# A two-layer hybrid encoder on one core: two gate/up tiles moved into the output projection, a norm weight moved to ScalarE, and the column halves of a product put in sequence

## The chip, the cores and the metric

The kernel runs on one core of a Trainium2 chip, in one launch, in float32. The metric is the device time of that core in microseconds, as the median of the runs. Matrix products run on TensorE (PE) with their weights loaded ahead of each matmul (PEld), results land in PSUM banks and are taken out by VectorE (DVE) or ScalarE (ACT). GpSimd (POOL) works on SBUF only, and SyncE (SP) issues most DMAs.

## The reference, cut to what matters

```python
for l in range(DEPTH):                                   # DEPTH = 2
    h = h + hybrid_mixer(rmsnorm(h, norm1_w[l]), ...)    # ends in: mix @ w_out
    h = h + swiglu(rmsnorm(h, norm2_w[l]), w_gate_up[l], w_down[l])
h = rmsnorm(h, final_norm_w)

def swiglu(h, w_gate_up, w_down):
    gate, up = jnp.split(h @ w_gate_up, 2, axis=-1)
    return (jax.nn.silu(gate) * up) @ w_down
```

The model width is 1024, the sequence 1024 plus 16 meta tokens, and gate and up are 2816 wide each. The change lies between the output projection of a layer (`mix @ w_out`) and the end of its gate/up products.

## The kernel before, in words

Activations are kept transposed: 128 channels on the partitions, tokens (1040 of them, 1024 in the last layer) along the free dimension. Every float32 operand is split in two float32r parts, hi and lo, and a product is three matmuls (hi by hi, hi by lo, lo by hi; lines 156 to 158 in `dense`, 1064 to 1066 in `prod`). For weights, ScalarE copies the raw tile to hi and GpSimd subtracts to get lo (lines 129, 130 in `wsplit`; 1046, 1047 in `w_op`).

**Output projection, second part.** `out_part(z, m)` adds one 128-channel block m of 8 for one half z of the token columns: 24 matmuls, two evacuations by VectorE (line 909, in `add_h`), a square on ScalarE and an add to the sums of the norm (line 954), and a store of the residual `hd`. `out_part(0, m)` runs for all m, then `out_part(1, m)`. Beside the latter, two blocks behind, VectorE forms the operands of the gate/up products.

**Gate and up as a Strassen-like product.** The operand (1024 channels by the tokens) is cut into four blocks B11, B21 (ready after z = 0) and B12, B22, and the weights of a tile f of 22 into A11, A12, A21, A22. Seven products follow: P1 (A11 B11), P2 (A12 B21), P3 (S4 B22), P4 (A22 T4), P5 (S1 T1), P6 (S2 T2), P7 (S3 T3). T1 to T4 are sums of the blocks, made by `t_sum` (line 981) and split into hi and lo by `t_split` (line 969) and `t_split_w` (line 177). S1 to S4 are sums of the weight blocks, made on VectorE for each tile (lines 1277, 1278, 1281, 1282). The norm weight of channels 0 to 511 in half z = 1 is multiplied in by a VectorE instruction of its own (line 1005).

**Early tiles.** P1 and P2 need only B11 and B21. For tiles 0 to 3 (`NE = 4`) they are done ahead, after all of the output projection, while VectorE finishes T1 to T4.

**The order within a tile.** In layer 0 the 520 columns of a half do not fit one bank, so each product runs twice (j = 0, 1) with 260 columns, 12 matmuls a time. The code runs all seven products for j = 0 and then all for j = 1. In the last layer one group of 12 matmuls of 512 columns is a product (`NJ = 1`). Bank c takes P5, is read by VectorE (line 1300), and then accumulates P3 on top. Bank b takes P6 (line 1314), P7 (line 1318) and P4 (line 1327) in this way, bank a P1 and P2. A product that accumulates therefore waits until VectorE has read the bank. After P4, gate and up are scaled and multiplied (line 1341 on GpSimd, 1342 and 1344 on VectorE).

**What sets the order.** A scheduler at build time places the instructions of each engine in one fixed order by the program's priorities and its own estimates; on the chip each engine then works through its list and waits by semaphores. So TensorE's list already interleaves products of neighbouring tiles. VectorE's list mixes evacuations with the sums of weights for the next tile.

Of the kernel before, what the change touches and what calls it, by code (L numbers as in the profile page):

```python
# [15 lines left out]
KT = 8  # L16
# [26 lines left out]
def trunk(ctx: ExitStack, tc: tile.TileContext, xT, w_in, w_ba, w_out, w_gu, w_dn,  # L43
# [235 lines left out]
    for l in range(DEPTH):  # L279
# [705 lines left out]
        X0, X1 = hb  # L985
        T = {}

        for m in range(KT):
            out_part(0, m)
            if m > 0:  # L990
                if m in (1, 5):
                    T[("B11", "B21")[m // 4]] = t_tile((Y[0][0], X[0][2])[m // 4])
                t_split_w(T[("B11", "B21")[(m - 1) // 4]], m - 1, 0)
        for m in range(KT + 2):
            if m < KT:
                out_part(1, m)
            if m == 0:
                t_split_w(T["B21"], 7, 0)
            k = m - 2
            if k < 0:  # L1000
                continue
            if k < 4:
                if k == 0:
                    T["T1"] = t_tile(Y[0][2])
                ts(out=hx(k, 1), in0=hx(k, 1), scalar1=pcol(P_N2 + k), scalar2=None, op0=ALU.mult)
                t_sum(k, 0, hx(k, 0), npar[:, k:k + 1], hx(k, 1), ALU.add)
                if k % 2:
                    t_split(T["T1"], X0, 0, k - 1)
            else:
                c = pcol(P_N2 + k)  # L1010
                if k == 4:
                    T["B22"] = t_tile(Y[0][1])
                t_split_w(T["B22"], k, 1)
                t_sum(k - 4, 1, hx(k, 1), c, hx(k - 4, 1))
                t_sum(k, 1, hx(k, 1), c, hx(k - 4, 0))
                t_sum(k, 0, hx(k, 0), c, hx(k, 1))
        T["T2"] = t_tile("P0")
        T["T3"] = t_tile("P1")
        for k in (0, 2):
            t_split(T["T2"], X1, 1, k)  # L1020
        for k in (0, 2):
            t_split(T["T3"], X0, 1, k)
        T["T4"] = t_tile(X[0][0])
        for k in (0, 2):
            t_split(T["T4"], X1, 0, k)

# [60 lines left out]
        NE = 4  # L1087
        early = {}
        for f in range(NE):
# [10 lines left out]
            for j in range(NJ):  # L1100
                prod(ab[j], w2, T["B21"], j, False)
                act(out=part(g, 0, j), in_=pin(ab[j]), func=AF.Copy)

# [163 lines left out]
        for f in range(FT):  # L1267
# [68 lines left out]
            else:  # L1336
                for j in range(NJ):
                    for p in (p1, p5, p3, p6, p7, p2, p4):
                        p(j)
# [214 lines left out]
```

## Time and profile before

| | us |
|---|---|
| median of 3 runs (2590.4 to 2598.9) | 2592.36 |
| profiled execution, its own time | 2589.49 |
| its span, first to last instruction | 2587.7 |
| TensorE busy | 2504.7 |
| VectorE busy | 1640.2 |
| GpSimd busy | 1134.3 |
| ScalarE busy | 1047.0 |

TensorE is busy for 97% of the span, so the time is that of its work plus its waits. The output projection's second half (z = 1) starts at 585.6 us in layer 0, the gate/up tiles run from there to about 1050 us; in the last layer the same stages lie from 1871.9 us to about 2360 us. In a row of a group, the numbers behind the bar are busy time and mean duration in ns, then the idle time just ahead and what ended it. In a row of waits they are the sum, the number of times and the longest.

### The profile page before, as it was taken

Reading aid. Unit: us, or ns where it says so; the run is one execution under the profiler, and the core shown is the slowest. Engines: PE = TensorE matmul, PEld = TensorE weight load, DVE = VectorE, ACT = ScalarE, POOL = GpSimd, SP = SyncE. Lnnn points to the kernel's source line nnn. Section 1 sums busy time; section 2 is a strip of 40 time slices with the busy share of each in tenths; the row PEclk is TensorE's granted clock in tenths of the full one; section 3 lists DMA queues with packets and bytes.
Section 4 is the critical chain, followed back from the end, with each engine's and each line's share of the span. In section 5 each row is a group of like instructions: output and inputs, shape, how many; then the busy total and the mean of one; then the engine's idle time right before and its main releaser. Section 6 shows DMA issues by size and latency. Waiting matters only on the chain. (4 is left out here: it accounts for less than half of the span.)

```text
span 2587.7 us, 45312 instructions
## 1 busy us (share of the span) xinstructions
PE 2504.7 (97%) x17508; PEld 2289.3 (88%) x17508; DVE 1640.2 (63%) x2461; ACT 1047.0 (40%) x1945; POOL 1134.3 (44%) x869
## 2 busy tenths in 40 slices
PE   8999999999899999999999989999989999999998
PEld 6989999998899999999998978999977778887787
DVE  4588433648766665778455874235587776668754
ACT  5563332435233333444445633324442333333444
POOL 2041212335666666665320302212456776774662
PEclk9999999999999999999999999999999999999999
DMA  3457265524422222674224582556343322228631
GB/s 127 128 184 266 92 206 167 186 78 124 131 98 87 96 83 81 212 221 144 78 92 134 189 269 77 181 159 204 106 133 115 111 88 92 89 82 276 202 109 66
DMA packets 213765, 360.04 MB, mean 139 GB/s; under 512 B 25461, under 2 KB 87869, under 8 KB 213549
## 3 DMA queue, kind: packets, MB, share of 16 engines
q1 hardware_dynamic: 180300, 310.17, 36.8%
q10 hardware_dynamic: 31072, 42.61, 5.4%
q0 software_dynamic: 2176, 4.36, 0.5%
q8 instruction: 137, 2.24, 0.4%
q14 instruction: 80, 0.65, 0.1%
HBM read 266.60 MB, written 90.46 MB: 138 GB/s over the span
## 5 line engine op out<-in xcount | busy, mean ns | idle before, releaser
L130 POOL TENSOR_TENSOR wlo<-raw,whi 128x512 fp32r<-128x512 f32 x132 | 177.5, 1346 | 770.2 <-ACT whi L129 698.4
L156 PE MATMUL pacc<-a,whi 128*128 128x346 f32 (+1 forms) x808 | 264.8, 331 | 9.9 <-ACT whi L129 8.3
L158 PE MATMUL pacc<-a,wlo 128*128 128x346 f32 (+1 forms) x808 | 264.5, 329 | 0.8 <-DVE wlo L130 0.8
L156 PE MATMUL pacc<-b,whi 128*128 128x346 f32 (+2 forms) x672 | 234.8, 350 | 0.0
L158 PE MATMUL pacc<-b,wlo 128*128 128x346 f32 (+2 forms) x672 | 232.5, 348 | 0.0
L157 PE MATMUL pacc<-a,whi 128*128 128x346 f32 (+1 forms) x688 | 227.0, 330 | 0.6 <-DVE a L177 0.3
L129 ACT ACTIVATE whi<-raw 128x512 fp32r<-128x512 f32 x168 | 105.2, 629 | 246.9 <-PE pacc L157 157.1
L157 PE MATMUL pacc<-b,whi 128*128 128x346 f32 (+2 forms) x580 | 200.5, 347 | 0.2 <-DVE b L905 0.2
L1047 POOL TENSOR_TENSOR wlo<-rw,whi 128x512 fp32r<-128x512 f32 x92 | 134.8, 1467 | 72.1 <-ACT whi L1046 66.8
L156 PEld LDWEIGHTS pacc<-a,whi 128*128 128x128 f32 x808 | 154.0, 191 | 13.9 <-ACT whi L129 10.2
L158 PEld LDWEIGHTS pacc<-a,wlo 128*128 128x128 f32 x808 | 154.1, 191 | 2.8 <-DVE wlo L130 1.4
L156 PEld LDWEIGHTS pacc<-b,whi 128*128 128x128 f32 x672 | 127.0, 189 | 11.4 <-issue 3.1
L157 PEld LDWEIGHTS pacc<-a,whi 128*128 128x128 f32 x688 | 131.8, 192 | 5.1 <-issue 2.9
L1047 POOL TENSOR_TENSOR a<-rw,a 128x512 fp32r<-128x512 f32 x64 | 105.6, 1651 | 69.7 <-ACT a L1046 69.0
L158 PEld LDWEIGHTS pacc<-b,wlo 128*128 128x128 f32 x672 | 126.9, 189 | 8.8 <-issue 0.8
L1047 POOL TENSOR_TENSOR b<-rw,b 128x512 fp32r<-128x512 f32 x64 | 92.6, 1449 | 84.2 <-ACT b L1046 50.2
L1046 ACT ACTIVATE whi<-rw 128x512 fp32r<-128x512 f32 x92 | 57.8, 630 | 144.5 <-DVE rw L1281 84.9
L157 PEld LDWEIGHTS pacc<-b,whi 128*128 128x128 f32 x580 | 109.6, 189 | 7.4 <-DVE b L905 0.5
L1282 DVE TENSOR_TENSOR rw<-raw,rw 128x512 f32<-128x512 f32 x44 | 97.2, 2209 | 1.2
L1277 DVE TENSOR_TENSOR rw<-rw,rw 128x512 f32<-128x512 f32 x44 | 67.5, 1533 | 47.3 <-POOL wlo L1047 30.9
L1047 POOL TENSOR_TENSOR wlo<-raw,whi 128x512 fp32r<-128x512 f32 x50 | 79.9, 1600 | 32.0 <-ACT whi L1046 21.3
L1046 ACT ACTIVATE b<-rw 128x512 fp32r<-128x512 f32 x64 | 40.2, 630 | 121.7 <-PE pacc L1065 35.2
(973 smaller groups left out, 8425.1 us busy)
## 6 DMA issues: line engine op xcount, KB each, us to landing
raw<-in_w_in SPq DMA_DIRECT2D x112, 256.0 KB
raw<-in_w_gu SPq DMA_DIRECT2D x104, 256.0 KB
rw<-in_w_gu SPq DMA_DIRECT2D x88, 256.0 KB
rw<-in_w_dn SPq DMA_DIRECT2D x86, 192.0 KB
rec<-aqd SPq DMA_DIRECT2D x62, 256.0 KB
rec<-vkd SPq DMA_DIRECT2D x61, 256.0 KB
raw<-in_w_out SPq DMA_DIRECT2D x48, 256.0 KB
b<-ad SPq DMA_DIRECT2D x45, 260.0 KB
```

The lines of the kernel that those rows point to most:

```text
L129: act(out=hi, in_=raw[:, 0:kk, :], func=AF.Copy)
L130: (tt if lov[0] else ptt)(out=lo, in0=raw[:, 0:kk, :], in1=hi.bitcast(F32), op=ALU.subtract)
L156: mm(ps[:, :n], wh, xh[:, n0:n1], start=(k == 0), stop=False)
L157: mm(ps[:, :n], wh, xl[:, n0:n1], start=False, stop=False)
L158: mm(ps[:, :n], wl, xh[:, n0:n1], start=False, stop=(k == K - 1))
L1046: act(out=hi, in_=src, func=AF.Copy)
L1047: ptt(out=lo, in0=src, in1=hi.bitcast(F32), op=ALU.subtract)
L1277: tt(out=s1t, in0=A21, in1=A22, op=ALU.add)
L1282: tt(out=A21, in0=A11, in1=A21, op=ALU.subtract)
```

## The change

Four edits, all between the output projection and the end of gate/up:

- The helper functions from `ad` to `pin` (unchanged) stand further up, and the body of the loop over early tiles becomes `early_tile(f)`. Tiles 0 and 1 are called in the loop over `out_part(1, m)`, right after m = 3 and m = 5. Tiles 2 and 3 stay where all four were.
- The norm weight (line 1005 before, 1087 after) is an activation with a scale on ScalarE.
- In a tile that is not the last, the loop over products is the outer one and the loop over column halves the inner one, and P2 stands ahead of P7.
- The split of A12 stands ahead of that of S3.

```diff
+        EARLY_AT = (3, 5)
+        def early_tile(f):
+            A11, A12 = raw4("raw"), raw4("raw")
+            dma(A11, w_gu[l, f, 0, :, 0:4, :])
+            dma(A12, w_gu[l, f, 0, :, 4:8, :])
+            w1, w2 = w_op(A11, True), w_op(A12, True)
...
         for m in range(KT + 2):
             if m < KT:
                 out_part(1, m)
+            if m in EARLY_AT:
+                early_tile(EARLY_AT.index(m))
...
-                ts(out=hx(k, 1), in0=hx(k, 1), scalar1=pcol(P_N2 + k), scalar2=None, op0=ALU.mult)
+                act(out=hx(k, 1), in_=hx(k, 1), func=AF.Copy, scale=pcol(P_N2 + k))
                 t_sum(k, 0, hx(k, 0), npar[:, k:k + 1], hx(k, 1), ALU.add)
...
-        for f in range(NE):
-            A11, A12 = raw4("raw"), raw4("raw")
...
+        for f in range(len(EARLY_AT), NE):
+            early_tile(f)
...
-                         [("S4", s2t), ("S3", A21), ("A12", A12), ("A22", A22)]):
+                         [("S4", s2t), ("A12", A12), ("S3", A21), ("A22", A22)]):
...
-                for j in range(NJ):
-                    for p in (p1, p5, p3, p6, p7, p2, p4):
+                for p in (p1, p5, p3, p6, p2, p7, p4):
+                    for j in range(NJ):
                         p(j)
```

Lines behind the moved block stand 7 further down in the changed kernel: 1277, 1278, 1281, 1282, 1300, 1311, 1314 become 1284, 1285, 1288, 1289, 1307, 1318, 1321, and 1318, 1327, 1342, 1344, 1347 become 1325, 1334, 1349, 1351, 1354.

What the scheduler makes of it is shown at three places on VectorE. The first is layer 0, where the last operands are done and tile 0 begins. The first piece is of the kernel before. P_ and a_671 are the splits of T2 to T4, rw tiles are sums of weights (6565 and 6558 of tile 0, 6736, 6737 and 6730 of tile 1), and a_680 is the up row of tile 0.

```order
L969 TENSOR_TENSOR a_671_6267<-a_511_5121,a_671_6267 128x1040 x2
L1278 TENSOR_TENSOR rw_6565<-rw_6564,raw_6556 128x512
L1282 TENSOR_TENSOR rw_6558<-raw_6556,rw_6558 128x512
L1281 TENSOR_TENSOR rw_6565<-raw_6557,rw_6565 128x512
L1277 TENSOR_TENSOR rw_6736<-rw_6730,rw_6731 128x512
L1278 TENSOR_TENSOR rw_6737<-rw_6736,raw_6728 128x512
L1282 TENSOR_TENSOR rw_6730<-raw_6728,rw_6730 128x512
L1300 TENSOR_TENSOR a_680_6286<-pacc_6588,a_680_6286 128x260
```

The same place of the changed kernel, where the up row of tile 0 is a_652.

```order
L1285 TENSOR_TENSOR rw_6565<-rw_6564,raw_6556 128x512
L1289 TENSOR_TENSOR rw_6558<-raw_6556,rw_6558 128x512
L981 SCALAR_TENSOR_TENSOR a_511_5121<-a_511_5121,par 128x520
L969 TENSOR_TENSOR P_690_6394<-a_511_5121,P_690_6394 128x1040
L969 TENSOR_TENSOR a_692_6404<-a_511_5121,a_692_6404 128x1040 x2
L1307 TENSOR_TENSOR a_652_6084<-pacc_6588,a_652_6084 128x260
L1307 TENSOR_TENSOR a_652_6084<-pf_6591,a_652_6084 128x260
L209 RECIPROCAL r_6550<-r_6550 128x260
L1288 TENSOR_TENSOR rw_6565<-raw_6557,rw_6565 128x512
L1284 TENSOR_TENSOR rw_6736<-rw_6730,rw_6731 128x512
```

The evacuation of P5 of tile 0 now stands ahead of the three sums for tile 1, and both halves of it together; two sums for tile 0 stand ahead of the last splits of T2 and T4.

The second place is the end of a tile in the steady part of layer 0, here of the tile with up row a_876 (f = 8), before the change. rw_8638 and rw_8632 are sums of weights two tiles on, and a_899 is the next tile's up row.

```order
L1327 TENSOR_TENSOR a_876_8194<-pb_8197,a_876_8194 128x260
L1277 TENSOR_TENSOR rw_8638<-rw_8632,rw_8633 128x512
L1282 TENSOR_TENSOR rw_8632<-raw_8630,rw_8632 128x512
L1318 TENSOR_TENSOR a_876_8194<-pb_8291,a_876_8194 128x260
L1300 TENSOR_TENSOR a_899_8431<-pacc_8433,a_899_8431 128x260
```

Before, every tile ends like this: the two sums stand between P4 of j = 0 and the evacuation of P7 of j = 1, and the next tile's P5 of j = 0 follows at once. In the changed kernel tiles end in two ways by turns. An odd tile (here f = 9, a_899):

```order
L1325 TENSOR_TENSOR a_899_8431<-pf_8434,a_899_8431 128x260
L1284 TENSOR_TENSOR rw_8873<-rw_8867,rw_8868 128x512
L1289 TENSOR_TENSOR rw_8867<-raw_8865,rw_8867 128x512
L1325 TENSOR_TENSOR a_899_8431<-pacc_8450,a_899_8431 128x260
L1334 TENSOR_TENSOR a_899_8431<-pf_8434,a_899_8431 128x260
```

An even tile (here f = 10, a_919; a_940 is the next one's up row):

```order
L1334 TENSOR_TENSOR a_919_8665<-pa_8668,a_919_8665 128x260
L1284 TENSOR_TENSOR rw_9107<-rw_9101,rw_9102 128x512
L1289 TENSOR_TENSOR rw_9101<-raw_9099,rw_9101 128x512
L1334 TENSOR_TENSOR a_919_8665<-pacc_8684,a_919_8665 128x260
L1285 TENSOR_TENSOR rw_9108<-rw_9107,raw_9099 128x512
L1349 TENSOR_TENSOR a_919_8665<-a_919_8665,rstd_5582 128x1040
L1351 TENSOR_TENSOR a_919_8665<-a_919_8665,a3f_8664 128x1040
L1307 TENSOR_TENSOR a_940_8900<-pacc_8902,a_940_8900 128x260
```

In the odd tile the two sums still stand ahead of an evacuation of P7, that of j = 1; in the even tile they and the product of gate and up stand ahead of the evacuation of the next tile's P5 of j = 0. On TensorE, between the end of P7 of j = 1 and the start of P4 of j = 1, 28 matmuls stand before the change and 28 in an odd tile after it; between the end of P4 of j = 0 and the next tile's P3 of j = 0, 71 stand in an even tile after it. In layer 1 TensorE's order of the products from tile 5 on is the same as before, but for one place where single matmuls of P2 and P3 change turns.

More of the change, by code (lines that the diff above doesn't have):

```diff
@@ L984, in trunk @@
         ts(out=npar, in0=par[:, l * P_L + P_N2:l * P_L + P_N2 + 4], scalar1=-1.0, scalar2=None, op0=ALU.mult)
[L985 to L1025, printed above, removed]
         ad = dram.tile([FT, 128, L], F32, name=nm("ad"))
```

39 lines of the change are left out of this document (added).

## The prediction

> **What bounds the kernel now.** I read the page first: which engine is busy, and how much of the span it isn't.
>
> ```profile
> span 2587.7 us, 45312 instructions
> ...
> PE 2504.7 (97%) x17508; PEld 2289.3 (88%) x17508; DVE 1640.2 (63%) x2461; ACT 1047.0 (40%) x1945; POOL 1134.3 (44%) x869
> ```
>
> TensorE's work is the time; the change takes no matmul away, so only TensorE's waits can move. Where these lie is told by the windows, cut at the stages. The columns are the stretch and its length, busy time of PE, PEld, DVE, ACT and POOL with counts, the granted clock, the DMA share and GB/s.
>
> ```profile
> 608.60:648.00 39.40, 32.92 (x246) 31.29 (x245) 34.16 (x39) 23.91 (x44) 23.30 (x14) 0.91 0.34 104
> 648.00:740.00 92.00, 84.44 (x689) 83.13 (x690) 68.90 (x93) 25.98 (x42) 56.68 (x35) 1.00 0.38 121
> 740.00:1045.00 305.00, 299.38 (x2467) 296.42 (x2466) 191.88 (x244) 100.38 (x176) 195.14 (x119) 1.00 0.25 86
> 1895.00:1932.60 37.60, 30.12 (x128) 22.12 (x129) 36.08 (x37) 21.59 (x34) 20.73 (x13) 1.00 0.32 102
> 1932.60:2060.00 127.40, 120.50 (x509) 95.97 (x509) 96.81 (x89) 39.70 (x61) 92.32 (x53) 0.99 0.37 121
> 2060.00:2350.00 290.00, 289.33 (x1250) 234.24 (x1249) 201.15 (x180) 97.03 (x156) 192.66 (x120) 1.00 0.31 104
> ```
>
> In layer 0 TensorE idles 6.5 us in the early tiles, 7.6 in tiles 0 to 3, and 5.6 in the 17 tiles after; in the last layer 7.5, 6.9 and 0.7. Together 34.8 us, and that caps any gain from waits. In the early stage of the last layer VectorE is busy for 36.1 of 37.6 us: there it is the bound. TensorE's waits name the releasers, here between 600 and 647 us.
>
> ```profile
> PE pacc L1064 <- DVE a L909: 2.5, 1, 2.5
> PE pf L1064 <- DVE a L909: 1.4, 1, 1.4
> PE pa L1066 <- POOL wlo L1047: 1.1, 1, 1.1
> PE pb L1064 <- ACT whi L1046: 1.0, 1, 1.0
> ```
>
> And from 740 to 1045 us:
>
> ```profile
> PE pacc L1064 <- DVE a L1318: 4.4, 11, 0.4
> PE pb L1064 <- DVE a L1318: 1.2, 3, 0.4
> ```
>
> The early tiles wait for VectorE to evacuate the output projection, which stands behind operand sums; a steady tile of layer 0 waits 0.4 us, once, for the evacuation of P7. In the last layer's steady tiles nothing is waited for.
>
> **Early stage, layer 0.** What could be had? The second half of the output projection and tile 0's P3 bound the stage on TensorE.
>
> ```profile
> 585.60 0.28 PE L158 MATMUL pacc<-o,wlo 128*128 128x260 f32 x1
> 648.07 0.39 PE L1064 MATMUL pacc<-b,whi 128*128 128x260 f32 x1 [0.41 <-DVE a L1300]
> ```
>
> Between them lie 192 matmuls of the projection, 192 of four early tiles and 48 of P5 and P6. At 299.38/2467 = 0.121 us each that is 52.4, so P3 could start at 638.0, about 10 us sooner. But what P3 waits for is VectorE, at line 1300, and VectorE's list says what is ahead of that.
>
> ```profile
> 616.82 0.75 DVE L909 TENSOR_TENSOR a<-pacc,a 128x260 f32<-128x260 f32 x2
> ...
> 634.01 3.47 DVE L969 TENSOR_TENSOR a<-a,a 128x1040 fp32r<-128x1040 f32 x2
> 637.41 0.68 DVE L1278 TENSOR_TENSOR rw<-rw,raw 128x512 f32<-128x512 f32 x1
> ...
> 647.59 0.42 DVE L1300 TENSOR_TENSOR a<-pacc,a 128x260 f32<-128x260 f32 x1
> 647.93 1.77 DVE L209 RECIPROCAL r<-r 128x260 f32<-128x260 f32 x1
> ```
>
> The last operand was split at 637.4. The four norm weights leave VectorE:
>
> ```profile
> L1005 DVE TENSOR_SCALAR a<-a,par x4: 491/836/1200, 592.3 to 606.0; 128x520 f32<-128x520 f32 x4
> L1005 DVE TENSOR_SCALAR b<-b,par x4: 486/1119/1186, 1878.2 to 1892.3; 128x512 f32<-128x512 f32 x4
> its engine sat idle before it (us, times) until:
>   DMA hd<-a: 3.0, 2
> ```
>
> In layer 0 four medians of 0.84 are 3.3 us less; the two sums of tile 0 that now stand ahead of the last splits are 2 times 0.68 more. VectorE is thus done at 635.5 at best. It may also be held by the evacuations: two early tiles, 96 matmuls or 11.6 us, now lie inside the projection, which before ended on TensorE at 608.6, so its last evacuation falls at about 620.4. Behind that stand the rest of the operands, 19.9 us before (from 617.5 to 637.4), now some 1.6 shorter since a sum and a split moved ahead: 638.7. Then come two evacuations (0.84), the reciprocal (1.77) and the S4 sum (0.68, which P3 needs), and the splits of S4 on ScalarE and GpSimd, some 1 to 2 us by the two shorter waits above: P3 starts at 640 to 644 against 648.07. I take 643, **a gain of 5 us**, since at 638.7 the later of the two paths decides; the ends are 0 and 8.6. The waits on line 909, 3.9 us of it, go, because the early tiles no longer stand behind the last evacuations; late next is S4.
>
> What these moves bring with them: ScalarE gets four instructions. An activation of that size with a scale stands in the stretch before:
>
> ```profile
> L176 ACT ACTIVATE b<-a,par 128x520 fp32r<-128x520 f32 x8 | 5.7, 715 | 0.0
> ```
>
> So 4 x 0.715 = 2.9 us, beside an engine that is busy for 23.9 of 39.4 us. They bring a wait along: before line 1005 VectorE sat idle 3.0 us there, in two waits for the store of `hd`. Behind it on ScalarE now stand weight splits and early evacuations, and TensorE waits for those; it costs nothing if TensorE still has projection blocks, and up to 3.0 us if not. On SP's queue, two loads of 256 KB per early tile now go ahead of projection weights; the DMA share there is 0.34, so I cost this at nothing. GpSimd makes four more lo parts in that time, busy 23.3 of 39.4. If this cover is gone, the waits of 1.0 and 1.1 us above come once more for each early tile, 4 us: that and the 3.0 make the end of 0 gain.
>
> **Early stage, last layer.** The same here, with VectorE the bound.
>
> ```profile
> 1920.04 3.45 DVE L969 TENSOR_TENSOR b<-b,b 128x1024 fp32r<-128x1024 f32 x2
> ...
> 1927.28 1.76 DVE L1281 TENSOR_TENSOR rw<-raw,rw 128x512 f32<-128x512 f32 x1 [1.52 <-POOL b L1047]
> ...
> 1932.65 0.40 PE L1064 MATMUL pb<-a,whi 128*128 128x512 f32 x1
> ```
>
> P3 starts at 1932.65, 3.6 us behind the S4 sum, which ends at 1929.0. Four norm weights (4 x 1.12 = 4.5 us) leave, two sums of 0.7 may come ahead, and the S4 sum follows the splits directly, at 1925 to 1926.6. P3 then starts about 4 us sooner: **gain 4**, ends 0 (VectorE's room is taken by late evacuations) and 7.5, the whole idle time.
>
> **Tiles 0 to 3 of layer 0** take 14.5 us each on TensorE (120 matmuls), VectorE is busy for 69 of 92 us. A bank that accumulates now has the other half's product in between, so waits for lines 1300 to 1318 shrink; VectorE's order keeps sums between evacuations. I take **2 of the 7.6 us**, ends -3 (as much as one more wait of a steady kind for each tile, and the refills) and +7.
>
> **Steady tiles of layer 0.** VectorE's durations, between 795 and 1045 us:
>
> ```profile
> L1282 DVE TENSOR_TENSOR rw<-raw,rw 128x512 f32<-128x512 f32 x12 | 33.7, 2810 | 0.4
> L1277 DVE TENSOR_TENSOR rw<-rw,rw 128x512 f32<-128x512 f32 x12 | 21.2, 1769 | 18.1 <-POOL wlo L1047 18.1
> L1342 DVE TENSOR_TENSOR a<-a,rstd 128x1040 f32<-128x1040 f32 x12 | 14.9, 1244 | 0.4
> L1344 DVE TENSOR_TENSOR a<-a,b3f 128x1040 f32<-128x1040 f32 x6 | 10.8, 1802 | 0.0
> ...
> L1278 DVE TENSOR_TENSOR rw<-rw,raw 128x512 f32<-128x512 f32 x13 | 9.0, 693 | 6.6 <-POOL a L1047 6.6
> ...
> L1327 DVE TENSOR_TENSOR a<-pacc,a 128x260 f32<-128x260 f32 x9 | 3.9, 428 | 2.4 <-PE pacc L1066 2.4
> ```
>
> Before, a tile waits 0.4 us plus the refill of the array (0.39 for the first matmul where the others take 0.28): 14 times 0.51 = 7.1 us. What replaces it follows from the two ways in which a tile now ends. Odd tile: from the end of P7 (j = 0) to P4 (j = 1), which needs P7's second half read, TensorE has 40 matmuls, 4.84 us. VectorE has 0.43 + 1.77 + 2.81 + 0.43 = 5.44 for L1325, L1284, L1289, L1325, and some 0.25, an estimate, for a matmul's end (0.28 long, begun every 0.12) and the signal: 0.85 late. Even tile: from the end of P4 (j = 0) to the next P3 (j = 0), TensorE has 71 matmuls, 8.6 us; VectorE has 0.43 + 1.77 + 2.81 + 0.43 + 0.69 + 1.24 + 1.80 + 0.43 and 0.25 = 9.85: 1.25 late. That holds if lines 1284 and 1289 stay at 1.77 and 2.81. Line 1278, the same operation on the same shape, takes 0.69; by that duration both would come 3.2 us sooner and no tile would wait.
>
> Why are they long? GpSimd is at work at the same time:
>
> ```profile
> 772.22 1.75 POOL L1047 TENSOR_TENSOR a<-rw,a 128x512 fp32r<-128x512 f32 x1
> ...
> 772.75 0.41 DVE L1318 TENSOR_TENSOR a<-pacc,a 128x260 f32<-128x260 f32 x1
> ```
>
> A sum of two SBUF operands beside GpSimd takes 1.8 to 2.8, an evacuation from PSUM beside it 0.41. The Trainium skill, page "SBUF — State Buffer", section "Who interferes with whom", says just this: a VectorE instruction with two SBUF inputs contends with a GpSimd instruction that reads SBUF, the shared ports being held for the whole instruction, and one with a single SBUF input doesn't; the rows agree. By it the sums stay long wherever GpSimd is busy beside them, and the steady tiles would come to the slower end below; were the lengths the sums' own place in the list instead, to the faster one.
>
> In the changed kernel the sums lie some 3 to 5 us later in the tile, GpSimd is busy 195 of 305 us, so about two thirds of the time. I take the odd tile in full and the even one at half (0.62): (0.85 + 0.62 + 2 x 0.11) x 8 pairs = 13.5, less 7.1: **6 us lost**. Ends: all waits gone, -7; both in full, (2.1 + 0.22) x 8 - 7.1 = +11.5. No wait for GpSimd ahead of L1284 is counted; before, it was 1.5 a tile (18.1 in 12), but the sum stands later now.
>
> **Steady tiles of the last layer**: from tile 4 on TensorE's list is the same but for one place, and so are its waits: 0. In its tiles 0 to 3 I take 0 as well, of 6.9.
>
> **Sum**, against the profiled execution of 2589.5 us: -5 - 4 - 2 + 6 = -5, so 2584.5. The median of the runs shown stands 2.9 above that execution, so **2587.4**.
>
> **Rivals.**
> - *Slower.* VectorE's L1284 and L1289 ahead of an evacuation that TensorE needs: all 16 steady tiles wait in full (+11.5), and, as VectorE stays the bound in layer 0's early stage, the 5 us there aren't had, nor the 2 behind it; the last layer gains 4 or nothing. 2592.4 + 11.5 - 4 = 2600 to 2604; I say 2602. It decides where the P5 evacuation (L1307) lands more than 8.6 us behind the end of P4 (j = 0). For it: all 12 of those sums were long before. Against it: GpSimd's list is reordered as well.
> - *Faster.* The waits go and nothing takes their place: early stages -8.6 and -4, tiles 0 to 3 -3, steady tiles 0. 2592.4 - 15.6 = 2577. For it: the longest waits, on line 909, lose their cause in the order itself. With the steady waits gone too it is 2570.
> - *The change doesn't do what it says.* Mixing frees TensorE only if VectorE is ahead; where VectorE sets the end of both early stages, TensorE's waits just move from line 909 to line 1307. Then only VectorE's own savings count, 3.3 - 1.4 and 4: with +6 this gives 2592.4, within the forecast.
>
> **How the numbers follow.** A measurement of this kernel can tell about 0.3%, 7.8 us, from no change: 2584.6 to 2600.2 counts as the same. The forecast, with the third rival, gets 0.40, the faster rival 0.34, the slower one 0.26. The range leaves out the faster rival's outer part and some mishap: 2573 to 2604.
>
> **What would show it.** Right: no waits of TensorE on `DVE a L909` in the early stage, P3 of tile 0 at about 643 where it was 648, the last-layer one 4 us sooner, waits on DVE L1325 and L1307 of about 1 us by turns in the steady tiles, and L1284 and L1289 at 1.8 and 2.8. Wrong: those two at 0.7 (then faster), or TensorE waiting for ScalarE's early evacuations or splits between 590 and 620 (then the stores' wait wasn't covered), or for weights of the projection (SP).

## The result and the profile after

The changed kernel takes 2596.13 us (median of 14 runs, 2590.57 to 2601.16) against 2592.65 for the kernel before: ratio 1.0011, 95% interval 1.0 to 1.0021. A second set of 11 runs gave 2594.47 and 1.0007 (0.9998 to 1.0016). That is within 0.3%, the class forecast as likeliest, and inside the range; but the forecast had it 5 us faster, and it came out 2 to 3 us slower. The ratios here and below leave out four runs that were far slower than all others (one of e9 with 4061 us, one of e11 with 2724 us, two of the kernel before with 3075 and 5636 us).

The page of the changed kernel, first lines:

```profile
span 2599.3 us, 45299 instructions
...
PE 2510.9 (97%) x17508; PEld 2294.5 (88%) x17508; DVE 1643.3 (63%) x2453; ACT 1049.3 (40%) x1953; POOL 1131.6 (44%) x869
```

The span is 11.6 us longer than that of the profiled execution before, far more than the medians. To see where, I cut every trace into stages at the starts of the same n-th matmuls: all traces have 17508, and outside the changed stages the order is the same but for a short piece at the start of layer 0's down projection. Four traces, two of each kernel (the second ones are the runs e5 and e13 below), in us:

| stage (numbers of its matmuls) | before | before, again | changed | changed, again |
|---|---|---|---|---|
| ahead of z = 1 of layer 0 (0 to 4524) | 579.3 | 579.3 | 583.6 | 577.7 |
| layer 0, z = 1 and early tiles (to 4980) | 65.1 | 64.2 | 63.0 | 61.9 |
| layer 0, first tiles (to 5592) | 81.2 | 80.2 | 81.8 | 84.4 |
| layer 0, steady tiles (to 8500) | 359.7 | 359.8 | 360.7 | 360.6 |
| between (to 14348) | 780.7 | 782.5 | 781.6 | 779.5 |
| last layer, z = 1 and early tiles (to 14650) | 57.7 | 56.1 | 54.8 | 53.0 |
| last layer, first tiles (to 15188) | 134.4 | 134.8 | 140.6 | 140.8 |
| last layer, steady tiles (to 16400) | 281.6 | 281.6 | 281.4 | 281.4 |
| last layer, to the last matmul | 235.7 | 241.0 | 239.4 | 240.9 |

The first, fifth and last rows hold the same instructions in both kernels; they differ by 2 to 6 us between executions of one kernel, and that is not the change. The cuts are numbers of matmuls, so the rows of the first tiles run on beyond tile 3, into tile 5 in layer 0 and tile 7 in the last layer. In the stages of the change, the early ones gain 2 to 3 us each, the first tiles give that back and more, the steady tiles of layer 0 lose 1. In sum 700.9 and 700.7 us (without the last layer's steady tiles) against 698.1 and 695.0: 3 to 6 us more, about what the medians say (2 to 3).

TensorE's waits, between 589 and 648 us of the changed kernel, the early stage of layer 0:

```profile
PE pb L1022 <- ACT a L1004: 1.3, 1, 1.3
PE pa L206 <- ACT b3f L1063: 0.9, 1, 0.9
PE pa L1022 <- ACT whi L1004: 0.8, 1, 0.8
PE pb L1024 <- POOL a L1005: 0.6, 1, 0.6
PE pf L158 <- POOL wlo L130: 0.5, 1, 0.5
```

The two waits on line 909 (3.9 us) are gone. New is the first row: P6 of tile 0 waits for ScalarE's split of S2. From 1876 to 1940 us, the early stage of the last layer:

```profile
PE pa L1022 <- ACT b L1004: 3.0, 1, 3.0
PE pacc L156 <- ACT whi L129: 2.4, 1, 2.4
PE pf L1022 <- DVE b L909: 1.7, 1, 1.7
PE pa L206 <- DVE rstd L954: 0.8, 1, 0.8
PE pacc L158 <- POOL wlo L130: 0.7, 1, 0.7
PE pacc L1024 <- POOL wlo L1005: 0.3, 1, 0.3
```

Here, too, P6 waits for S2 (first row), and 2.4 + 0.7 us go to splits of a projection weight. The 2.4 us are a price of the moved norm weight in this execution. ScalarE's timeline shows it, the number in brackets being the idle time ahead and what ended it:

```profile
1893.41 0.72 ACT L1087 ACTIVATE b<-b,par 128x512 f32<-128x512 f32 x1 [2.46 <-DMA hd<-b]
1894.04 0.61 ACT L129 ACTIVATE whi<-raw 128x512 fp32r<-128x512 f32 x1
```

The norm weight waits 2.46 us for the store of `hd`, and the split (line 129) that TensorE needs stands right behind it.

What holds P6? First VectorE, then ScalarE and TensorE in layer 0:

```profile
641.14 2.38 DVE L969 TENSOR_TENSOR a<-a,a 128x1040 fp32r<-128x1040 f32 x2
643.44 0.42 DVE L1307 TENSOR_TENSOR a<-pacc,a 128x260 f32<-128x260 f32 x1
```
```profile
643.56 1.15 ACT L1004 ACTIVATE a<-rw 128x512 fp32r<-128x512 f32 x2 [1.51 <-DVE a L969]
```
```profile
589.96 0.28 PE L158 MATMUL pacc<-o,wlo 128*128 128x260 f32 x1
```
```profile
644.24 0.39 PE L1022 MATMUL pb<-P,a 128*128 128x260 f32 x1 [1.34 <-ACT a L1004]
...
649.88 0.42 PE L1024 MATMUL pb<-P,a 128*128 128x260 f32 x1
```
```profile
650.10 0.42 PE L1022 MATMUL pacc<-b,whi 128*128 128x260 f32 x1
```

S2 goes into the ring of weight buffers, which lies in the storage of the residual's channels 512 to 1023 (`big(X[0][1])` in `wslot`). The last split of T4 (641.14, two instructions, to 643.5) still reads that storage, so ScalarE's split starts at 643.56, and P6 at 644.24. P3 follows at 650.10, 60.1 us behind the start of z = 1 (589.96); before, 62.5 (585.60 to 648.07). In the last layer P6 starts here, behind the same split:

```profile
1935.00 0.78 PE L1022 MATMUL pa<-P,b 128*128 128x512 f32 x1 [2.99 <-ACT b L1004]
```
```profile
1931.93 2.35 DVE L969 TENSOR_TENSOR b<-b,b 128x1024 fp32r<-128x1024 f32 x2
```

This matmul has the number 14652. So in the last layer the cut at 14650 lies just ahead of the wait, and the table puts it to the first tiles; in layer 0 P6 (4942) and P3 (4966) lie ahead of the cut at 4980. It is safer to add the two rows of a layer. Of the 6 us that the first tiles of the last layer lose, P6 makes 5: from matmul 14650 to P3's first (14664) it is 8.4 us against 3.2, the wait and a granted clock of 0.62 behind it (1935.0 to 1939.5 us). Further on, one wait takes the place of another. The first of these rows is of the kernel before, the second of the changed kernel:

```profile
1943.51 0.79 PE L1064 MATMUL pa<-P,b 128*128 128x512 f32 x1 [2.36 <-DVE a L1314]
```
```profile
1968.36 0.47 PE L1022 MATMUL pacc<-a,b 128*128 128x512 f32 x1 [3.02 <-DVE b L1307]
```

### The profile page after: what moved, and what is told of

It is laid out like the page before. It is cut to its first block, busy times and chain, and to the rows that moved or that the text cites. A ratio compares the mean times of both kernels' runs of the same rounds, so it can differ in the third digit from the quotient of the medians.

```text
span 2599.3 us, 45299 instructions
## 1 busy us (share of the span) xinstructions
PE 2510.9 (97%) x17508; PEld 2294.5 (88%) x17508; DVE 1643.3 (63%) x2453; ACT 1049.3 (40%) x1953; POOL 1131.6 (44%) x869
## 5 line engine op out<-in xcount | busy, mean ns | idle before, releaser
L130 POOL TENSOR_TENSOR wlo<-raw,whi 128x512 fp32r<-128x512 f32 x132 | 176.7, 1340 | 775.1 <-ACT whi L129 702.5
L1005 POOL TENSOR_TENSOR wlo<-rw,whi 128x512 fp32r<-128x512 f32 x126 | 187.8, 1497 | 80.1 <-ACT whi L1004 63.1
L129 ACT ACTIVATE whi<-raw 128x512 fp32r<-128x512 f32 x168 | 105.2, 628 | 250.5 <-PE pacc L157 170.7
L1004 ACT ACTIVATE whi<-rw 128x512 fp32r<-128x512 f32 x126 | 78.8, 630 | 192.6 <-DVE rw L1288 53.4
L1005 POOL TENSOR_TENSOR a<-rw,a 128x512 fp32r<-128x512 f32 x47 | 72.9, 1554 | 100.9 <-ACT a L1004 61.0
L1005 POOL TENSOR_TENSOR b<-rw,b 128x512 fp32r<-128x512 f32 x47 | 67.6, 1441 | 82.4 <-ACT b L1004 51.7
L295 DVE TENSOR_TENSOR a<-pacc,rstd 128x346 f32<-128x346 f32 (+2 forms) x59 | 32.7, 554 | 82.0 <-PE pacc L158 81.8
L1289 DVE TENSOR_TENSOR rw<-raw,rw 128x512 f32<-128x512 f32 x44 | 82.1, 1866 | 1.2
L1237 DVE TENSOR_TENSOR P<-a,P 128x512 fp32r<-128x512 f32 x63 | 59.9, 977 | 26.7 <-ACT P L1236 21.0
L1237 DVE TENSOR_TENSOR P<-b,P 128x520 fp32r<-128x520 f32 x63 | 59.1, 971 | 27.4 <-ACT P L1236 27.4
```

The costliest lines, as they stand in the source:

```text
L129: act(out=hi, in_=raw[:, 0:kk, :], func=AF.Copy)
L130: (tt if lov[0] else ptt)(out=lo, in0=raw[:, 0:kk, :], in1=hi.bitcast(F32), op=ALU.subtract)
L1004: act(out=hi, in_=src, func=AF.Copy)
L1005: ptt(out=lo, in0=src, in1=hi.bitcast(F32), op=ALU.subtract)
L1237: tt(out=lo, in0=r, in1=hi.bitcast(F32), op=ALU.subtract)
L1289: tt(out=A21, in0=A11, in1=A21, op=ALU.subtract)
```

## The experiments

**Theories.** *A:* the norm weight stalls ScalarE's list on the store of `hd`, and splits that TensorE needs queue behind it. *B:* VectorE's room decides: what it has to do up to the end of the last operand split sets when tile 0 can go on. *C:* the mix moves the last evacuations back, so the last split comes late, and the early tiles, already done, no longer cover the wait for it and for the ring.

All ratios are to the kernel before, with their 95% intervals. The sum is of the layer 0 stages from z = 1 to the end of the steady tiles, and the last layer's from z = 1 to the end of its first tiles, from one trace (before: 698.1 and 695.0; changed: 700.9 and 700.7). The end of the last split (line 969) is counted from the start of matmul 4524 and of matmul 14348.

| run | mix | norm weight | order | median us | ratio | sum us | last split, layer 0 / last |
|---|---|---|---|---|---|---|---|
| before | - | DVE | old | 2592.65 | 1 | 698.1 | +52.4 / +51.8 |
| e5 before, again | - | DVE | old | 2593.65 (one run) | - | 695.0 | +51.3 / +50.2 |
| changed | 2 tiles | ACT | new | 2596.13 | 1.0011 [1.0, 1.0021] | 700.9 | +54.0 / +57.7 |
| e13 changed, again | 2 tiles | ACT | new | 2594.47 | 1.0007 [0.9998, 1.0016] | 700.7 | +54.4 / +55.9 |
| e1 | 2 tiles | DVE | new | 2596.61 | 1.0022 [1.0007, 1.0037] | 700.6 | +57.7 / +54.9 |
| e2 | - | ACT | old | 2602.91 | 1.0051 [1.0039, 1.0063] | 703.7 | +48.5 / +46.7 |
| e3 | 2 tiles | DVE | old | 2599.28 | 1.0036 [1.0023, 1.005] | 701.6 | +55.8 / +55.5 |
| e4 | - | DVE | new | 2603.6 | 1.0055 [1.0038, 1.0072] | 705.7 | +51.4 / +52.7 |
| e9 | 2 tiles | ACT | old | 2594.84 | 1.0003 [0.9991, 1.0015] | 697.3 | +54.5 / +54.1 |
| e15 | - | ACT | new | 2607.81 | 1.0061 [1.0049, 1.0073] | 705.4 | +48.5 / +46.9 |
| e6 | 2 tiles | left out | new | 2594.13 | 0.9996 [0.9986, 1.0005] | 697.1 | +53.5 / +54.2 |
| e7 S2 not in the ring | 2 tiles | ACT | new | 2596.78 | 1.0005 [0.9992, 1.0017] | 698.0 | +54.1 / +57.5 |
| e8 | 1 tile | ACT | new | 2595.49 | 1.0004 [0.9992, 1.0016] | 695.4 | +54.8 / +51.8 |
| e12 | 1 tile | DVE | new | 2599.36 | 1.0019 [1.0009, 1.003] | 703.6 | +56.3 / +55.0 |
| e10 reciprocal late | 2 tiles | ACT | new | 2600.62 | 1.0027 [1.0014, 1.0039] | 700.4 | +54.2 / +52.8 |
| e11 e7, e8 and e10 in one | 1 tile | ACT | new | 2599.88 | 1.0025 [1.0015, 1.0036] | 702.3 | +54.3 / +53.0 |
| e14 lo of T3, T4 twice | 2 tiles | ACT | new | 2608.57 | 1.0062 [1.0048, 1.0076] | 712.2 | +61.7 / +61.9 |

Two things are to be seen before the single runs. Every edit by itself costs 0.36 to 0.55%, and the whole costs 0.1%: the edits are not additive. And the end of the last split answers to the edits as the mechanism says (the norm weight off VectorE without the mix: 3 to 5 us sooner; the mix: 3 to 5 us later), while the time does not follow it alone.

**e1**, against the changed kernel:

```diff
-                act(out=hx(k, 1), in_=hx(k, 1), func=AF.Copy, scale=pcol(P_N2 + k))
+                ts(out=hx(k, 1), in0=hx(k, 1), scalar1=pcol(P_N2 + k), scalar2=None, op0=ALU.mult)
```

> The changed kernel with the norm weight back on VectorE (mix and product order stay). Theory A, ScalarE's list stalls: the moved norm weight waits for the store of hd, weight splits queue behind it, and TensorE's waits on the splits of the projection's weights (2.4 us on whi L129 and 0.7 us on wlo L130 in the last layer) go; the stage from the projection's second half to tile 4 is 3 us shorter in the last layer than in the changed kernel, 0 to 2 shorter in layer 0, and the time is 2591 to 2594, 3 to 5 below the changed kernel. Theory B, VectorE's room decides: four instructions of 0.8 to 1.1 us go back to it in each layer, the last operand split comes 3 to 4 us later, and the time is 2599 to 2604.

Both missed on the time. The waits on whi L129 in the last layer went, and its stages were 3.1 us shorter than in the changed kernel's first trace, as A expects; in layer 0 the last split came 3.7 us later and the stages were 2.8 longer, as B expects. But against the second trace of the changed kernel (e13) the two are only 1.5 and 1.3 us, within the scatter of these stages: the signs fit A in one layer and B in the other, and neither is shown by this run.

**e2, e3, e4** and **e15** do parts of the change on the kernel before: the line of e1 in reverse; `early_tile` and its two calls; the two lists below; the first and the last.

```diff
-                         [("S4", s2t), ("S3", A21), ("A12", A12), ("A22", A22)]):
+                         [("S4", s2t), ("A12", A12), ("S3", A21), ("A22", A22)]):
...
-                for j in range(NJ):
-                    for p in (p1, p5, p3, p6, p7, p2, p4):
+                for p in (p1, p5, p3, p6, p2, p7, p4):
+                    for j in range(NJ):
```

> The kernel before with only the norm weight moved to ScalarE. Theory A: the wait for the store is taken over to ScalarE and TensorE waits for splits of the projection's weights, but the last operand split comes up to 3 us sooner and pays for it: 2590 to 2596. Theory B: only the gain is left, both layers 3 to 4 us shorter: 2585 to 2588.

Both theories missed: 0.5% slower, though the last split came 3 to 5 us sooner. TensorE's waits between 600 and 640 us are a part of it:

```profile
PE pa L1064 <- ACT whi L1046: 3.8, 1, 3.8
PE pa L1066 <- POOL wlo L1047: 3.5, 1, 3.5
PE pacc L1064 <- DVE a L909: 2.7, 2, 2.2
```

In the kernel before the rows for ScalarE and GpSimd were 1.0 and 1.1. ScalarE's timeline has the reason:

```profile
628.07 1.07 ACT L968 ACTIVATE P<-a 128x1040 fp32r<-128x1040 f32 x1 [3.29 <-DVE a L981]
629.22 1.07 ACT L968 ACTIVATE a<-a 128x1040 fp32r<-128x1040 f32 x1
630.20 0.61 ACT L1046 ACTIVATE whi<-raw 128x512 fp32r<-128x512 f32 x1
```

The split of an early tile's weights (630.20) stands behind hi parts of T2 to T4 (line 968), and ScalarE sits idle 3.29 us ahead of these for VectorE's sums. So the order of ScalarE's list, not its load, is behind the first row. The second row comes of GpSimd's lo part of the same weights, which follows the hi part and takes 4.22 us; the same operation took 1.77 and 2.17 us at about this place of the kernel before:

```profile
630.88 4.22 POOL L1047 TENSOR_TENSOR wlo<-raw,whi 128x512 fp32r<-128x512 f32 x1 [4.08 <-ACT whi L1046]
```

> The kernel before with only the two early tiles moved into the projection. Theory A: without ScalarE's stall the waits on L909 go and the stage is 2 to 4 us shorter in layer 0; in the last layer the gain is taken by the sums and the reciprocal that the order puts ahead of the last operand splits (some 4 us), so 0 to +2 there: 2588 to 2592. If the mix itself is the loss (theory C: early tiles spent ahead of time no longer cover the last splits), the last layer is 3 us or more longer, as in the changed kernel, and the time is 2594 to 2600.

The early stages gained 1.6 and 5.0 us and the first tiles lost 3.7 and 6.1 against the first trace of before. In the last layer that is 1 to 2 us longer in all, not the 3 us or more that C called for, though the time lies in C's range; A's 2 to 4 us of gain in layer 0 is not there once the first tiles are counted. What C does get is its place: P6 waits 2.9 us for S2 here with the mix alone. That wait is 2.8 to 3.0 us in all runs with two early tiles moved and nothing else done about the split or the ring (both traces of the changed kernel, e1, e3, e6, e9), and none of the runs without the mix or with one early tile (before, e5, e2, e4, e15, e8, e12, e11) has one over 0.4 us at this place.

> The kernel before with only the order of products and splits changed (halves in sequence, P2 ahead of P7, A12 ahead of S3). Theories A and C: layer 0's steady tiles change by -1 to +2 us as in the changed kernel (its waits on L1318 turn to waits on ScalarE's splits L1046 and a few on L1300), the last layer by 0: 2591 to 2595. By the prediction's price for steady tiles (+6) it is 2598.

The steady tiles are as A and C expect (360.0 against 359.7), yet it is 0.55% slower, 14 us, which no theory had. The first tiles of layer 0 take 7 us of it, 88.4 against 81.2. The waits there, 643 to 742 us, are for VectorE's evacuations; the four longest rows:

```profile
PE pf L1064 <- DVE c L1318: 2.9, 1, 2.9
PE pacc L1064 <- DVE c L1300: 2.6, 1, 2.6
PE pacc L1064 <- DVE a L1300: 1.8, 2, 1.3
PE pb L1064 <- DVE a L1318: 1.6, 1, 1.6
```

All rows together are 10.5 us, and such waits were 7.9 us in the kernel before (647 to 740 us). So they make some 3 of the 7 us; about as much goes with the granted clock, 0.97 over these 99 us, where the kernel before had 1.00.

> The kernel before with the norm weight on ScalarE and the new order, without the mix: the last corner. If each edit has a price of its own, that is 13 + 14 us: 2610 to 2620. If the losses come from the same few waits (what ScalarE and VectorE happen to have queued when tile 0 begins) it is 5 to 15 us: 2599 to 2608. If the two together are within 3 us of the kernel before, the mix is not what makes the whole neutral.

The middle case: 15 us more, not 27. The order adds next to nothing to the norm weight alone (the first tiles of layer 0 take 82.7 us here, 82.6 in e2, against 88.4 with the order alone): the waits between 643 and 742 us are 6.5 us here and 10.5 with the order alone. That the sooner splits are the reason is likely, but not shown.

**e9** is the changed kernel with e4's lists undone.

> The changed kernel with the old order of products and splits; the mix and the norm weight on ScalarE stay. It says what the order is worth inside the full change. Theory: the order does nothing in the steady tiles (one wait of 0.9 us for each pair of tiles in place of two of 0.56), and shifts only where VectorE's sums stand in tiles 0 to 3 of layer 0, where the mix with the old order lost 3.8 us against 1.0 with the new one: so 2 to 4 us more than the changed kernel, 2597 to 2601, all of it in tiles 0 to 3 of layer 0. Rival: the order is a loss of its own, as its 12 us in the kernel before would have it, and this kernel is faster than the changed one, 2588 to 2592.

Neither case came. The mix and the norm weight together cost nothing that can be measured, and the order adds nothing to it that can be (1.0011 against 1.0003, overlapping). The first tiles of layer 0 take 83.9 us, between the changed kernel's two traces (81.8 and 84.4), so the expected 2 to 4 us can't be told from scatter. The last layer's early stage is 51.4 us against 54.8 in the first trace of the changed kernel: the wait on whi L129 is 0.3 there, with the norm weight on ScalarE all the same and ScalarE idle 4.3 us ahead of it for the store. So A's stall is on the path in one trace and nearly off it in another.

**e6** leaves the norm weight out (the line of e1 deleted).

> The changed kernel with the norm weight of channels 0 to 511 in half z = 1 left out, on either engine, so that those channels enter T1 to T4 without it. Theory A, ScalarE's stall on the store: the waits on whi L129 of 2 us in the last layer go, its early stage is 3 us shorter than the changed kernel's, as with the weight on VectorE, and the time falls to 2591 to 2594. Theory C, early tiles spent too soon: the 6 us that tiles 0 to 3 lose in the last layer stay, since the last operand split and the buffers that it frees are still late. If they go too, the norm weight is the cause of both.

Each theory has its part. As A says, the waits on whi L129 are gone and the last layer's early stage is shorter, 51.4 us against 54.8 and 53.0; as C says, the first tiles there still take 139.7, and P6 still waits:

```profile
1930.10 0.50 PE L1022 MATMUL pa<-P,b 128*128 128x512 f32 x1 [2.95 <-ACT b L1004]
```

By the sums of single traces the norm weight costs 3 to 4 us on either engine (700.9, 700.7 and 700.6 against 697.1), which is near their scatter; it is not what the first tiles of the last layer lose.

**e13** is the changed kernel once more.

> The changed kernel, unchanged, for a second profile and more times. If ScalarE's stall on the store costs TensorE every time, the wait of 2.4 us on whi L129 and a last projection matmul 39 us behind the start of z = 1 in the last layer are here again, and the stage there is 3 us longer than the kernel before's; if it is chance, the last projection matmul is at 34 to 36 us, as with the mix and the norm weight alone, and that stage is within 1 us of the kernel before. Time 2594 to 2598 either way.

Chance for a part: the wait on whi L129 is 1.4 us, the last projection matmul comes at +36.1, and the early stage is 53.0. What came back unchanged is P6 in the last layer:

```profile
1926.39 0.50 PE L1022 MATMUL pa<-P,b 128*128 128x512 f32 x1 [2.98 <-ACT b L1004]
```

**e7** puts S2 of the first tile elsewhere:

```diff
-            if i in (0, 2, 4):
+            if i in (0, 2, 4) or (wn[0] == 2 and not early):
```

> The changed kernel with S2 of tile 0 split into the rotating weight buffers and not into the ring, which lies in the storage of the residual's channels 512 to 1023 and is free only after the last split of T4. Theory C (ring): TensorE's wait ahead of P6 (1.3 us in layer 0, 3.0 us in the last) goes or shrinks below 1 us, with the half-rate stretch behind it, and tile 0 to 3 is 3 to 5 us shorter in the last layer, 2 in layer 0: 2588 to 2592. Rival (VectorE's list decides): the wait only moves to P3 or P7, and the time stays within 1 us of the changed kernel's 2596.

Waits of TensorE from 1920 to 1940 us:

```profile
PE pacc L1022 <- ACT b L1004: 2.6, 1, 2.6
PE pb L1022 <- ACT b L1004: 0.9, 1, 0.9
PE pa L1024 <- POOL wlo L1005: 0.5, 1, 0.5
```

The rival: ahead of P6 there is no ring any more, and instead of 3.0 us TensorE waits 0.9 for the next product and 2.6 for a later one, whose weights are again in the ring. The trace's sum is 2.9 us less, the median is the same.

**e8** (`EARLY_AT = (3,)`) and **e12** (that with e1's line):

> The changed kernel with only one early tile in the projection, three behind it. Theory C: with one more tile as cover for the last splits the wait ahead of P6 is gone or under 1 us in both layers, while one of the waits on L909 comes back (1.4 to 2.5 us): 2591 to 2595, between the kernel before and the changed one or below both. Rival: each mixed tile costs by itself, then the loss of the last layer's tiles 0 to 3 is half of the 6 us.

> One early tile in the projection and the norm weight on VectorE. Theory A: with one tile mixed there is less behind the norm weight on ScalarE's list, so its stall matters less than with two; VectorE gets 3.3 and 4.5 us back and the last splits come 2 to 4 us later: 2595 to 2599, as fast or slower than with the weight on ScalarE. Rival: the stall is the main loss in any mix, and this is 2 to 4 us faster than one early tile with the weight on ScalarE.

With three tiles behind the projection the last layer's first tiles take 134.4 us, as before the change, and no wait ahead of P6 is left: cover it is, as C says. Both rows of the last layer together are 188.8 us, against 195.4 and 193.8 in the changed kernel and 192.1 and 190.9 before. The wait on line 909 that C expected did not come back. But splits of an early tile's weights are waited for again (1.2 us on ScalarE and 0.9 on GpSimd in the last layer, 4.1 and 1.8 us on ScalarE in layer 0), and the median is the changed kernel's. In e12 the last splits came 1.5 and 3.2 us later than in e8, and it was slower (1.0019 against 1.0004, with intervals that overlap), as theory A had it.

**e10** issues the sums of the norm and the reciprocal at the end of tile 0, and **e11** joins e7, e8 and e10.

```diff
-        finish_bc(ss, o0, L, rsd[0])
...
+            if f == 0:
+                finish_bc(ss, o0, L, rsd[0])
```

> The changed kernel with the sums of the norm and the reciprocal (1.74 us on VectorE, L209) issued at the end of tile 0 and not ahead of the last operand splits. Theory: the end of the last split follows what VectorE has to do behind the last evacuation, so in the last layer it comes 1.7 us sooner (57.7 us behind the start of z = 1 in the changed kernel), and the wait ahead of P6 falls from 3.0 to about 1.3; in layer 0, where the reciprocal already stands behind the splits, nothing: 1 to 3 us faster than the changed kernel, 2593 to 2595. Rival: another sum takes the place, no change.

> One early tile in the projection, the reciprocal late, and S2 of tile 0 in the rotating buffers: the three that helped or should. By the sum of their parts in the traces (last layer -3.4 against the kernel before, layer 0 about 0) 2588 to 2592, 0 to 4 below the kernel before and the fastest so far; if the waits only move among VectorE's and ScalarE's lists, as for S2 alone, 2593 to 2597.

Both missed: 0.27 and 0.25% slower, above every range given. In e10 the wait ahead of P6 fell to 1.9 us, and 50 us later in the last layer one of 5.4 us for ScalarE's split appears. Parts that each helped in a trace did not add up.

**e14** repeats the instruction that forms lo, for T3 and T4:

```diff
-            tt(out=lo, in0=s, in1=hi.bitcast(F32), op=ALU.subtract)
+            for _ in range(n):
+                tt(out=lo, in0=s, in1=hi.bitcast(F32), op=ALU.subtract)
```

> The changed kernel with VectorE's four instructions that form the lo parts of T3 and T4 done twice in each layer, with the same values: some 5 us more for VectorE ahead of the end of the last split. Theory (what VectorE has to do behind the last evacuation sets when tile 0 can go on): the last split ends 5 us later, and the kernel is 7 to 11 us slower than the changed one, 2602 to 2607. Rival (TensorE has other work there): below 3 us.

The last splits ended 7.5 and 5.1 us later than the mean of the two traces of the changed kernel, and the early stage and first tiles took 8.0 and 4.3 us more. (In layer 0 it is more than 5, since an evacuation and the reciprocal, 2.1 us, now stand ahead of the last splits too.) The time is above the theory's range: 14 us more than e13, of which these stages have 12. TensorE waits just there:

```profile
647.07 0.58 PE L1023 MATMUL pb<-P,a 128*128 128x260 f32 x1 [8.13 <-ACT a L1005]
```
```profile
1945.04 0.79 PE L1023 MATMUL pa<-P,b 128*128 128x512 f32 x1 [5.29 <-ACT b L1005]
```

So, with the mix, the end of the last split sets when tile 0 goes on, about one to one, as B says for this place. **e5** is the kernel before for a second profile:

> The kernel before, unchanged, for a second profile. It shows how far the stages that the change doesn't touch move from one execution to the next: the first 585 us (the changed kernel took 4.4 us more there) and the down projection of the last layer (3.7 to 7.3 us more in all five other kernels). If the 4 us wait at about 2450 us is in this profile too, it is chance and not the change; if this one waits 1.4 us as in the first profile, the changed stages reach that far.

The wait in the down projection is 3.9 us there, and was 1.4 in the first:

```profile
2456.07 0.77 PE L1411 MATMUL pa<-P,whi 128*128 128x512 f32 x1 [3.94 <-DVE b L1417]
```

So the 4 to 7 us at the end, in all the other traces, were luck of the first profile and no reach of the change.

**What stays open.** A trace's stages scatter by 1 to 3 us between executions of one kernel, so the 2 to 3 us by which the changed kernel is slower can't be given to one edit. And the norm weight, or the order, by itself costs more than the traces' sums say (13 and 14 us against 7 and 9). A part of that shows in the granted clock that is on record for each run. Its mean was 0.9868 over the six runs of e2 and 0.9912 over the twelve of the kernel before beside them; 0.0044 of 2600 us are 11 us, an estimate of what the lower clock can cost if TensorE is at work all the while. For the order alone it is 0.9888, by the same working 6 of the 14 us; for e15 0.9860 against 0.9910, 13 of 15 us; for the changed kernel beside the same runs (e13) 0.9891, 5 us, more than it lost. So waits seem to cost twice, once by themselves and once by the half-rate stretch behind them, and how many such stretches an execution has differs. No run sets the clock apart from the waits, so this stays an argument.

## Why the prediction was wrong

- *What bounds.* Right in that TensorE is busy for 97% of both spans. But its work was taken as fixed: with the same 17508 matmuls it is busy for 2510.9 us against 2504.7, at a granted clock of 0.988 against 0.991. The stretches at half rate that stand behind waits had no term in the sum.
- *Early stage of layer 0, 5 us.* Its rule held: VectorE done with the operands 53.1 us behind the start of z = 1 (638.7 - 585.6), measured 53.5 (643.5 - 589.96). P3 came 2.3 us sooner (3.1 in e13), not 5. What was put behind the split, two evacuations, the reciprocal and the S4 sum, was wrong. S2's split, not S4's, is late next, since it waits for the ring's storage, and P6's 24 matmuls then ran at half rate. This window of the changed kernel has the granted clock third from the end:

```profile
641.00:645.60 4.60, 1.86 (x15) 1.00 (x15) 3.69 (x6) 2.56 (x6) 1.33 (x2) 0.91 0.27 92
645.60:651.20 5.60, 5.60 (x26) 5.60 (x27) 4.39 (x5) 2.30 (x4) 4.20 (x4) 0.50 0.31 77
```

- *Early stage of the last layer, 4 us.* **This is the step that failed.** "The same here, with VectorE the bound": I took the 4.5 us that leave VectorE off the end of the last split and didn't bound that end by the last evacuation, as I had a paragraph earlier for layer 0. Before, that split ended at 1923.5; P3 started at 1932.65 and now starts at 1939.72, of which 4.86 are from earlier stages: 2.2 us later, not 4 sooner. The last evacuation moves from 32.0 us behind the start of z = 1 to 42.3 (40.5 in e13; 39.9 with the mix alone, e3), and behind it stand some 15 us of operands, two sums and the reciprocal, so the split ends at +57.7 and not at +51.8. TensorE then waits 3.0 us ahead of P6 for the ring that the split frees, and runs at half rate behind it. The bound was within reach before: the projection's last matmul stood at +22.9, and 48 matmuls of two early tiles at 0.232 us (290.00 / 1250) put it at +34.0, 2 us behind the old last evacuation. With the 19.8 us of VectorE's work that stood behind that one (51.8 - 32.0), the split could come no sooner than before. The two rows of this layer came out 3.3 and 2.9 us longer, where -4 was forecast: 7 us of the miss.
- *Tiles 0 to 3.* Forecast -2 in layer 0 and 0 in the last; measured +0.6 and +6.2 by the first traces, +4.2 and +6.0 by the second. I had read the last layer's tiles off TensorE's list, which is nearly the same from tile 4 on, and had priced tiles 0 to 3 at nothing though that list doesn't speak for waits. e3, e8 and e14 show where 5 of the 6 us come from: the same late split, and the ring that it frees.
- *Steady tiles of layer 0, +6.* The waits are at the two places that were named, and the sizes were off. (So was the count: the 7.1 us taken off were those of 14 tiles, the loss that of 16; alike it is +5.) They were 1.25 us ahead of P3 in even tiles and 0.85 ahead of P4 in odd ones; measured:

```profile
PE pacc L1022 <- ACT a L1004: 4.5, 6, 0.8
PE pacc L1022 <- DVE a L1307: 0.9, 1, 0.9
```

  0.75 us for each pair, all on the place of P3, and 0.1 at P4. Six of the seven are put down to ScalarE and not to line 1307, but the two end together (at 782.58 and 782.52 in the tile below), so which of them holds P3 isn't settled. The sum is +1.0 (360.7 and 360.6 against 359.7 and 359.8), so the waits were exchanged about one for one. VectorE's timeline in an even tile:

```profile
773.78 1.27 DVE L1284 TENSOR_TENSOR rw<-rw,rw 128x512 f32<-128x512 f32 x1
775.08 0.69 DVE L1289 TENSOR_TENSOR rw<-raw,rw 128x512 f32<-128x512 f32 x1
775.69 0.42 DVE L1334 TENSOR_TENSOR a<-pacc,a 128x260 f32<-128x260 f32 x1
776.03 1.45 DVE L1285 TENSOR_TENSOR rw<-rw,raw 128x512 f32<-128x512 f32 x1
777.40 2.33 DVE L1349 TENSOR_TENSOR a<-a,rstd 128x1040 f32<-128x1040 f32 x1
779.83 2.35 DVE L1351 TENSOR_TENSOR a<-a,a3f 128x1040 f32<-128x1040 f32 x1
782.10 0.42 DVE L1307 TENSOR_TENSOR a<-pacc,a 128x260 f32<-128x260 f32 x1
```

  And GpSimd's:

```profile
775.51 1.42 POOL L1005 TENSOR_TENSOR a<-rw,a 128x512 fp32r<-128x512 f32 x1 [1.01 <-ACT a L1004]
776.94 1.68 POOL L1005 TENSOR_TENSOR a<-raw,a 128x512 fp32r<-128x512 f32 x1
779.78 1.30 POOL L1005 TENSOR_TENSOR wlo<-rw,whi 128x512 fp32r<-128x512 f32 x1 [1.16 <-ACT whi L1004]
```

  The sums for the next tiles (the first two rows of VectorE) took 1.96 us and not 4.58; the three operations behind them, on lines 1285, 1349 and 1351, took 6.13 and not 3.73. Line 1289 ran mostly while GpSimd was idle and took 0.69; the two multiplies, with GpSimd at work beside them, took 2.33 and 2.35, where they took 1.24 and 1.80 before. (Means of all tiles from 800 to 1045 us: 1.30 and 1.75 for lines 1284 and 1289, where 1.77 and 2.81 were taken over from before, and 1.83 and 2.23 for the multiplies.) What is stretched is whatever of two SBUF operands lies beside GpSimd's work, not a line of the program: the long times moved from one group to the other. That is the Trainium skill's rule ("SBUF — State Buffer", "Who interferes with whom") and the trace agrees. To price a moved instruction by its old duration was the mistake.
- *ScalarE's wait for the store, 0, with an end of 3.0.* The end was nearer in the changed kernel's two traces (2.4 + 0.7 and 1.4 + 0.7), the choice in e9 (0.3 + 0.4).
- *Sum and chances.* -5 for a measured +2 to +3. In layer 0 the terms add up to -1, and the traces have -0.5 and +2.7: the first of these is near by luck, since too much gain in the early stage and too much loss in the steady tiles cancel. The third rival, that TensorE's waits only move from line 909 elsewhere and the time stays (2592.4), came closest; I had counted it into the forecast's class and not made it the forecast.

## What to carry to other kernels

Where an engine works up to the end of a stage, taking work from it or filling another engine's wait moves that end only if the last input comes sooner: find the last input of the last step in each stage, in each layer anew, and bound by it. Work that was done "too late" may be the cover of something later; ask what it covers before moving it ahead. An edit that costs nothing in a whole can cost 0.5% by itself, so try single edits out in their company.

## What the runs showed of the hardware

- A stretch of half clock (granted 0.50 for 5.6 us) followed a window of 4.6 us (641.0 to 645.6 us of the changed kernel) in which TensorE was busy for 1.86 us with no single wait over 1.34 us; the waits of 0.75 us in the steady tiles, one in 42 us, were followed by none (granted clock 1.00 from 744 to 1050 us).
- Executions of one kernel differ by 5 us in stages where the instructions are the same (235.7 and 241.0 us for the last one, both of the kernel before).
